# Table loads with buffers and a queue to themselves in a hybrid attention, RWKV-7 and PEER kernel

## The chip, the cores and the metric

The kernel runs on one core of a Trainium2 chip. The metric is the device time in microseconds, as the median of several timed executions; lower is better. One more execution was taken with the hardware profiler. Every number of the trace is from that one.

## What is computed

Two layers of a transformer-like backbone over 512 latent tokens and 256 context tokens of 1024 features. Each layer first mixes tokens (windowed attention, neighbourhood attention and RWKV-7 scans in parallel head groups, one projection out), then runs a PEER layer, which is what this case is about. The PEER layer, cut to what matters:

```python
q = (hb @ wq).reshape(PEER_CHUNK, PEER_HEADS, 2, PEER_QDIM // 2)
s = jnp.einsum('thpd,hpnd->thpn', q, sub_keys).astype(jnp.float32)
sv, si = lax.top_k(s, PEER_TOPK)                 # 16 of 128 keys, twice for each of 8 heads
cand = (sv[:, :, 0, :, None] + sv[:, :, 1, None, :]).reshape(PEER_CHUNK, PEER_HEADS, PEER_TOPK * PEER_TOPK)
best, ci = lax.top_k(cand, PEER_TOPK)            # 16 of the 256 pairs
expert = i1 * PEER_NKEYS + i2                    # one of 128 * 128 experts
gate = jax.nn.softmax(best, axis=-1)
ue = jnp.take(u, expert, axis=0)
ve = jnp.take(v, expert, axis=0)
act = jax.nn.gelu(jnp.einsum('td,thkd->thk', hb, ue).astype(jnp.float32), approximate=False)
return jnp.einsum('thk,thkd->td', (gate * act).astype(hb.dtype), ve)
```

Each token takes 8 x 16 = 128 of the 16384 experts, each a row of the table u and a row of the table v.

## The kernel before

**Two ways to the same sum.** Most tokens are treated densely: the product of all 16384 experts with the token tile is formed and weighted by a matrix W that is zero where an expert was not chosen. In layer 0 these are the four latent tiles of 128 tokens, in layer 1 three of them. The other tiles (the two context tiles in layer 0, the last latent tile in layer 1) are gathered: for each of a token's 128 experts an indirect DMA fetches 128 rows, one per token, of u and v side by side (8 KB each, 1 MB a gather), VectorE forms the dot product with the token (L1472), ScalarE the Gelu (L1474), VectorE multiplies by the gate (L1475) and accumulates v (L1478). Two gathers make one step of this kind (`NQ = 2`). `Gather.tick` is called at fixed places of the dense loops and issues as many gathers as `NTICK` gives for the place, with a high priority: entry 0 in the scores, 1 and 2 in the scored stage, for the first `NFIRST` groups and for the rest, 3 in the value stage.

**The scored stage** (`scored`, called 32 times per layer, a group of four blocks of 128 experts each). A uT row of 1 MB holds two blocks. ScalarE casts a block to its high half (L1311), VectorE subtracts for the low half (L1313), TensorE makes three products per chunk of features into `pa` (`mm3`, L132 to L134: 24 matmuls a block, 512 columns in layer 0, 384 in layer 1), ScalarE applies Gelu (L1317), and the result `aw` is written to the DRAM scratch `ascr` (L1319). Blocks near the end are kept in SBUF instead (`keep`) and multiplied at once by their part of W, a gate row read back from the scratch `wscr` (L1300, L1322): groups 24 to 31 in layer 0, 21 to 31 in layer 1. The half-cast blocks have two buffers each.

**W** is made during the scored stage by `gates`, a generator of five units per dense tile: one of preparation, four that each make W for 32 tokens in eight steps. A step is two one-hot comparisons and one product on VectorE (L1225, L1228), eight matmuls (L1233) and a copy on ScalarE (L1234). At its end a unit writes W, 2 MB, to `wscr` (L1236); W has one buffer. The units are dealt evenly over the first `GSPREAD` groups. In layer 0, `mod_unit` computes one sixth of the next layer's modulation after each fifth group, with four rows of weights each (L167) and matmuls (L159).

**The value stage** runs over the same 128 blocks, kept ones first: a row of v for two blocks (L1364), the same high and low split (L1367, L1369), for blocks not kept `ascr` and `wscr` are read back (L1357, L1359) and multiplied (L1374), and TensorE accumulates into `py` (18 or 24 matmuls of 512 columns a block).

**Rows and queues.** One pool of `NROW` buffers of 8 KB per partition (`Gather.row`) serves the gathers, the tables uT and uv, the gate rows, the modulation rows, the weights of the score stages (L1107), the context's output projection and `load_out`, and the residual rows at the end of a layer. All of these but the gathers are loaded by DMAs that SyncE (SP) issues; so are the writes of `ascr` and `wscr`. Gathers are issued by GpSimd (POOL). A queue is in order: an instruction that waits for its buffer or its data holds everything behind it. The order on each engine, and which free buffer a tile gets, is set when the program is built, by a scheduler that simulates a timeline; no order is written by hand.

## Time and profile before

| | us |
|---|---|
| timed, median of 3 | 5024.15 (5021.28 to 5025.62) |
| profiled execution, its own time | 5011.65 |
| its span, first to last instruction | 5009.9 |
| TensorE matmuls busy | 4425.2 (88%) |
| VectorE busy | 3653.8 (73%) |
| ScalarE busy | 1772.4 (35%) |
| GpSimd busy | 1226.5 (24%) |

The expert stages take about half of the span: layer 0's scored stage from 1096 to 2123 us, its value stage to about 2850, layer 1's scored stage from 3662 to 4464 and its value stage to the end. Busy time says that an engine had an instruction under way; for matmuls the end is modelled, so a count of matmuls times the spacing of an undisturbed stretch tells more. Idle time of an engine is put down to what ended it. The granted clock (PEclk) is TensorE's, as a share of full speed; the DMA share is how much of the 16 DMA engines' time was in use.

### The profile page before, as it was taken

The page shows a single profiled execution, that of the slowest core. Times are in us where ns is not written, and L with a number is a line of the kernel's source. Part 1 is how long each engine was busy: PE and PEld are TensorE (multiplying, and loading weights), DVE is VectorE, ACT ScalarE, POOL GpSimd, SP SyncE. Part 2 cuts the span into 40 slices and gives each one's busy share as a digit, 9 for nine tenths or more (in the row PEclk, how much of TensorE's full clock was granted, in tenths as well). Part 3 has the DMA queues.
Part 4 walks back from the last instruction along what each step waited for, and adds up shares of the span by engine and source line. Part 5 has one row for each costly group of instructions (what it writes and reads, how often), then busy time and mean ns, then how long its engine had stood idle before and what let it go on. Part 6 is the DMA issues. An engine that isn't in the chain of part 4 may idle for free.

```text
span 5009.9 us, 74083 instructions
## 1 busy us (share of the span) xinstructions
PE 4425.2 (88%) x27525; PEld 3669.7 (73%) x27525; DVE 3653.8 (73%) x7587; ACT 1772.4 (35%) x2961; POOL 1226.5 (24%) x1347
## 2 busy tenths in 40 slices
PE   7778887789999988899999886799698997999999
PEld 4557776667787776677788664777588996988787
DVE  3974666889877876677788878557579875676776
ACT  3533245333333332222232354335334332333333
POOL 0025632151112222222222115354031110111120
PEclk9788797899999998999999987889899998999999
DMA  7444654255778888887999834573526885886897
GB/s 268 149 113 124 175 174 157 101 190 199 272 288 340 335 310 309 320 305 274 334 373 351 286 117 120 129 202 103 176 92 219 323 296 223 289 307 251 310 328 243
DMA packets 573481, 1186.55 MB, mean 237 GB/s; under 512 B 62768, under 2 KB 376000, under 8 KB 520384
## 3 DMA queue, kind: packets, MB, share of 16 engines
q1 hardware_dynamic: 506688, 758.39, 45.0%
q0 software_dynamic: 61440, 418.41, 22.6%
q10 hardware_dynamic: 4992, 5.02, 0.4%
q8 instruction: 216, 3.54, 0.3%
q14 instruction: 145, 1.19, 0.1%
HBM read 1005.19 MB, written 176.50 MB: 236 GB/s over the span
## 4 chain that ended last, share of the span: by engine, by line
PE 45%; DVE 16%; issue 15%; DMA 15%; POOL 4%; ACT 3%; SPq 1%; POOLq 0%; ACTq 0%; DVEq 0%
DMA row<-in_uv,eidx 6%; PE py L133 5%; PE py L132 4%; PE py L134 4%; PE pa L132 4%; PE pa L134 4%; PE pa L133 4%; PE pw L1233 3%; DMA row<-in_uT 3%; PE pf L132 2%; POOL row L1461 2%; PE pf L133 2%; PE pf L134 2%; DVE uL L1313 1%; PE pg L840 1%
## 5 line engine op out<-in xcount | busy, mean ns | idle before, releaser
L1461 POOL DMA_INDIRECT row<-in_uv,eidx x384 | 547.4, 1426 | 2350.1 <-DVE accc L1478 1153.0
L132 PE MATMUL pa<-hH,uH 128*128 128x512 f32 (+1 forms) x2048 | 772.8, 377 | 81.9 <-ACT uH L1311 68.0
L134 PE MATMUL pa<-hH,uL 128*128 128x512 f32 (+1 forms) x2048 | 764.6, 374 | 21.1 <-DVE uL L1313 21.0
L133 PE MATMUL pa<-hL,uH 128*128 128x512 f32 (+1 forms) x2048 | 762.8, 372 | 0.0
L133 PE MATMUL py<-vL,GH 128*128 128x512 f32 x1792 | 699.8, 392 | 19.8 <-DVE vL L1369 19.6
L134 PE MATMUL py<-vH,GL 128*128 128x512 f32 x1792 | 697.1, 391 | 0.0
L132 PE MATMUL py<-vH,GH 128*128 128x512 f32 x1792 | 684.3, 392 | 13.3 <-ACT vH L1367 9.2
L1472 DVE SCALAR_TENSOR_TENSOR row<-row,h2c 128x1024 f32<-128x1024 f32 x384 | 473.6, 1236 | 230.3 <-DMA row<-in_uv,eidx 229.8
L132 PEld LDWEIGHTS pa<-hH,uH 128*128 128x128 f32 x2048 | 399.5, 195 | 138.9 <-ACT uH L1311 79.0
L1478 DVE SCALAR_TENSOR_TENSOR accc<-row,dt,accc 128x1024 f32<-128x1024 f32 x384 | 494.2, 1287 | 5.7
L1311 ACT CAST uH<-row 128x1024 fp32r<-128x1024 f32 x256 | 266.2, 1049 | 570.1 <-PE pa L133 435.7
L134 PEld LDWEIGHTS pa<-hH,uL 128*128 128x128 f32 x2048 | 397.4, 194 | 74.6 <-DVE uL L1313 32.7
L1313 DVE TENSOR_TENSOR uL<-row,uH 128x1024 fp32r<-128x1024 f32 x256 | 311.6, 1222 | 161.4 <-ACT uH L1311 156.4
L133 PEld LDWEIGHTS pa<-hL,uH 128*128 128x128 f32 x2048 | 398.8, 195 | 40.1
L133 PEld LDWEIGHTS py<-vL,GH 128*128 128x128 f32 x1792 | 338.6, 189 | 97.2 <-DVE vL L1369 26.9
L132 PEld LDWEIGHTS py<-vH,GH 128*128 128x128 f32 x1792 | 339.2, 189 | 86.0 <-ACT vH L1367 10.0
L134 PEld LDWEIGHTS py<-vH,GL 128*128 128x128 f32 x1792 | 338.8, 189 | 70.0
L1369 DVE TENSOR_TENSOR vL<-row,vH 128x1024 fp32r<-128x1024 f32 x256 | 311.5, 1220 | 13.4 <-ACT vH L1367 13.1
L1367 ACT CAST vH<-row 128x1024 fp32r<-128x1024 f32 x256 | 266.4, 1044 | 15.5 <-DMA row<-in_uv 13.5
L1225 DVE TENSOR_TENSOR oh<-iota,ix 128x512 f16<-128x512 f16 x448 | 171.9, 421 | 135.5 <-PE pw L1233 135.1
L1233 PE MATMUL pw<-og,oh 128*128 128x128 f16 x1792 | 237.9, 297 | 36.4 <-DVE og L1228 19.2
L1233 PEld LDWEIGHTS <-oh 128*128 128x128 f16 x1792 | 190.4, 119 | 76.6 <-DVE og L1228 35.1
(380 smaller groups left out, 8352.1 us busy)
## 6 DMA issues: line engine op xcount, KB each, us to landing
row<-in_uT SPq DMA_DIRECT2D x128, 1024.0 KB
row<-in_uv SPq DMA_DIRECT2D x128, 1024.0 KB
wscr<-W SPq DMA_DIRECT2D x28, 2048.0 KB
wmod<-in_w_mod SPq DMA_DIRECT2D x48, 512.0 KB
row<-in_wq SPq DMA_DIRECT2D x24, 1024.0 KB
ascr<-aw SPq DMA_DIRECT2D x96, 256.0 KB
row<-in_w_mod SPq DMA_DIRECT2D x24, 1024.0 KB
av<-ascr SPq DMA_DIRECT2D x48, 512.0 KB
```

The lines of the kernel that those rows point to most:

```text
L132: mm(out, lh, rh, start=first, stop=False)
L133: mm(out, lh, rl, start=False, stop=False)
L134: mm(out, ll, rh, start=False, stop=last)
L1225: nc.vector.tensor_tensor(oh[:, z], self.iota4, ix[:, z, tt].unsqueeze(1).to_broadcast([P, P, 4]), OP.is_equal)
L1233: nc.tensor.matmul(pw[:, q], oh[:, 1, :, q], og[:, z, :, q], start=z == 0, stop=z == 1)
L1311: nc.scalar.copy(uH, ur)
L1313: nc.vector.tensor_tensor(uL, ur, uH.bitcast(F32), OP.subtract)
L1367: nc.scalar.copy(vH, vr)
L1369: nc.vector.tensor_tensor(vL, vr, vH.bitcast(F32), OP.subtract)
L1461: self.K.nc.gpsimd.indirect_dma_start(out=r, out_offset=None, in_=self.K.i[f"uv{self.l}"], in_offset=bass.IndirectOffsetOnAxis(ap=self.idx ...
L1472: nc.vector.scalar_tensor_tensor(rows[z][:, 0:D], rows[z][:, 0:D], 1.0, self.h[:, a], OP.mult, OP.mult, accum_out=dt[:, z:z + 1])
L1478: nc.vector.scalar_tensor_tensor(acc, v, dt[:, z:z + 1], acc, OP.mult, OP.add)
```

## The change

Five things. The tables uT and uv get two row buffers of their own (`table`), and the common rows go from six to four. The loads of gate rows and of modulation rows are issued by GpSimd, and the writes of `ascr` and `wscr` by ScalarE, all of them by SyncE before. The gate product of a gathered pair moves from one VectorE instruction to two ScalarE ones. The units of W are dealt over 19 groups instead of 22 in layer 0 and 15 instead of 18 in layer 1. And the gathers per tick are set anew: in layer 0 fewer in the scored stage and more in the value stage, with ten instead of twelve groups at the low rate; in layer 1 in the same direction. What is computed stays the same.

```diff
--- before.py
+++ after.py
@@ -33,10 +33,11 @@
 NMIX, NFFN, CV, W0, A0, KKC, KAC, RKC = 0, 8, 16, 61, 69, 77, 81, 85
 NCOL = 89
 LATER = 2000
-NROW = 6
+NROW = 4
+NTAB = 2
 NQ = 2
 MOFF = 500
-GSPREAD = (22, 18)
+GSPREAD = (19, 15)
 LATE = (28, 28)
 NRAW = 4
 TC0 = 6
@@ -54,8 +55,8 @@
 NPRT = 4
 NQKB = {"qs": 3, "kh": 3, "kl": 2}
 
-NTICK = ((2, 1.2, 2.6, 1.75), (0, 0, 1.3, 0.9))
-NFIRST = (12, 3)
+NTICK = ((2, 1.2, 2.3, 1.9), (0, 0, 1.2, 1.0))
+NFIRST = (10, 3)
 FEATS = (12, 13, 4, 0, 5, 1, 6, 2, 7, 3, 14, 8, 9, 10, 11)
 LAT = (0, 1, 2, 3)
 
@@ -164,7 +165,7 @@
             else:
                 if k % 2 == 0:
                     w2 = row().rearrange("p (k n) -> p k n", k=2)
-                    nc.sync.dma_start(w2, src[:, k:k + 2])
+                    nc.gpsimd.dma_start(w2, src[:, k:k + 2])
                 w = w2[:, k % 2]
             for j in range(4):
                 add(j, self.cs[:, k], w[:, j * 256:j * 256 + 256], k == 0, False)
@@ -1233,7 +1234,7 @@
                         nc.tensor.matmul(pw[:, q], oh[:, 1, :, q], og[:, z, :, q], start=z == 0, stop=z == 1)
                 nc.scalar.activation(W[:, :, t4 * 4:t4 * 4 + 4], pw.rearrange("p q i -> p i q"), AF.Copy,
                                      scale=1.0 / GSCALE)
-            nc.sync.dma_start(self.wscr[:, 4 * t + s_], W)
+            nc.scalar.dma_start(self.wscr[:, 4 * t + s_], W)
             yield
 
     def peer_norm(self, l, np_, j, mc, hH, hL, tiles, ps, gat):
@@ -1297,10 +1298,10 @@
 
                 if 4 * g >= P - nres - LATE[l]:
                     wt = gat.row()[:, :4 * nd].rearrange("p (a q t) -> p a q t", q=4, t=32)
-                    nc.sync.dma_start(wt, self.wscr[:, :nd // 32, g * 4:g * 4 + 4, :])
+                    nc.gpsimd.dma_start(wt, self.wscr[:, :nd // 32, g * 4:g * 4 + 4, :])
                 for b in range(4 * g, 4 * g + 4):
                     if b % 2 == 0:
-                        ur2 = gat.row().rearrange("p (z k n) -> p z k n", z=2, k=KC)
+                        ur2 = gat.table().rearrange("p (z k n) -> p z k n", z=2, k=KC)
                         nc.sync.dma_start(ur2, i["uT"][l, b:b + 2].rearrange("z p k n -> p z k n"))
                     if b >= P - nres - (LATE[l] if late else 0):
                         aw = keep[b] = (ar if b >= P - nres else late).tile([P, nd], F32, name=f"ar{b}")
@@ -1316,7 +1317,7 @@
                         self.mm3(pa, uH[:, k], uL[:, k], hH[:, k, :nd], hL[:, k, :nd], k == 0, k == KC - 1)
                     nc.scalar.activation(aw, pa, AF.Gelu)
                     if b not in keep:
-                        nc.sync.dma_start(self.ascr[g, :, b % 4, :nd], aw)
+                        nc.scalar.dma_start(self.ascr[g, :, b % 4, :nd], aw)
                     else:
                         a3 = aw.rearrange("p (a t) -> p a t", t=32)
                         nc.vector.tensor_tensor(a3, a3, wt[:, :, b % 4], OP.mult)
@@ -1360,7 +1361,7 @@
                 for q in range(4):
                     b = g * 4 + q
                     if b % 2 == 0:
-                        vr2 = gat.row().rearrange("p (z d) -> p z d", z=2)
+                        vr2 = gat.table().rearrange("p (z d) -> p z d", z=2)
                         nc.sync.dma_start(vr2, vtab[b * P:(b + 2) * P, :].rearrange("(z p) d -> p z d", p=P))
                     vr = vr2[:, b % 2]
                     vH = vp.tile([P, D], F32R, name="vH", bufs=3)
@@ -1456,6 +1457,9 @@
     def row(self):
         return self.gp.tile([P, 2 * D], F32, name="row", bufs=NROW)
 
+    def table(self):
+        return self.gp.tile([P, 2 * D], F32, name="tab", bufs=NTAB)
+
     def gather(self, a, k):
         r = self.row()
         self.K.nc.gpsimd.indirect_dma_start(out=r, out_offset=None, in_=self.K.i[f"uv{self.l}"],
@@ -1472,7 +1476,8 @@
             nc.vector.scalar_tensor_tensor(rows[z][:, 0:D], rows[z][:, 0:D], 1.0, self.h[:, a], OP.mult, OP.mult,
                                            accum_out=dt[:, z:z + 1])
         nc.scalar.activation(dt, dt, AF.Gelu)
-        nc.vector.tensor_tensor(dt, dt, self.gate[:, a, k:k + NQ], OP.mult)
+        for z in range(NQ):
+            nc.scalar.activation(dt[:, z:z + 1], dt[:, z:z + 1], AF.Copy, scale=self.gate[:, a, k + z:k + z + 1])
         for z in range(NQ):
             v, acc = rows[z][:, D:2 * D], self.acc[:, a]
             nc.vector.scalar_tensor_tensor(acc, v, dt[:, z:z + 1], acc, OP.mult, OP.add)
```

## Rows read from the trace of the kernel before

**Rows 1.** Stretches: busy us (count) of PE, PEld, DVE, ACT, POOL; PEclk, DMA share, GB/s.

```profile
1160.00:1870.00 710.00, 676.10 (x3556) 544.60 (x3557) 568.04 (x1180) 234.77 (x375) 133.22 (x92) 0.97 0.79 296
1870.00:2123.00 253.00, 199.78 (x919) 153.65 (x917) 161.16 (x214) 55.58 (x89) 57.49 (x42) 0.89 0.88 316
2123.00:2500.00 377.00, 355.77 (x1518) 290.89 (x1519) 280.15 (x375) 105.43 (x161) 86.50 (x60) 0.97 0.85 303
2500.00:2826.00 326.00, 326.00 (x1440) 269.93 (x1439) 270.82 (x357) 97.04 (x145) 70.74 (x52) 1.00 0.98 356
3780.00:4200.00 420.00, 390.95 (x2344) 371.65 (x2343) 352.72 (x709) 158.73 (x256) 71.57 (x48) 0.96 0.78 285
4200.00:4270.00 70.00, 44.38 (x273) 40.44 (x273) 32.79 (x62) 18.06 (x29) 1.94 (x2) 0.71 0.54 200
4270.00:4464.00 194.00, 178.97 (x965) 174.08 (x963) 132.84 (x175) 59.04 (x93) 33.08 (x27) 0.95 0.83 299
```

**Rows 2.** The same stretches, instructions of `pa` alone: PE, PEld, ACT.

```profile
1160.00:1870.00 710.00, 546.37 (x2226) 424.80 (x2227) 54.47 (x93) 0.97 0.79 296
1870.00:2123.00 253.00, 188.32 (x773) 149.38 (x771) 19.62 (x33) 0.89 0.88 316
...
3780.00:4200.00 420.00, 324.90 (x1695) 302.85 (x1694) 34.11 (x71) 0.96 0.78 285
4200.00:4270.00 70.00, 27.86 (x145) 26.80 (x145) 2.92 (x6) 0.71 0.54 200
4270.00:4464.00 194.00, 178.97 (x965) 174.08 (x963) 19.31 (x40) 0.95 0.83 299
```

**Rows 3.** The page's costliest groups: busy, mean ns, idle before and what ended it.

```profile
L1478 DVE SCALAR_TENSOR_TENSOR accc<-row,dt,accc 128x1024 f32<-128x1024 f32 x384 | 494.2, 1287 | 5.7
...
L1313 DVE TENSOR_TENSOR uL<-row,uH 128x1024 fp32r<-128x1024 f32 x256 | 311.6, 1222 | 161.4 <-ACT uH L1311 156.4
...
L1225 DVE TENSOR_TENSOR oh<-iota,ix 128x512 f16<-128x512 f16 x448 | 171.9, 421 | 135.5 <-PE pw L1233 135.1
...
L1233 PEld LDWEIGHTS <-oh 128*128 128x128 f16 x1792 | 190.4, 119 | 76.6 <-DVE og L1228 35.1
```

**Rows 4.** Groups by line and form, whole span: one-hot product, Gelu, gate product.

```profile
L1228 DVE TENSOR_TENSOR og<-oh,g 128x1024 f16<-128x1024 f16 x224 | 151.7, 686 | 0.0
...
L1474 ACT ACTIVATE dt<-dt 128x2 f32<-128x2 f32 x192 | 38.8, 202 | 479.2 <-DVE row L1472 479.0
...
L1475 DVE TENSOR_TENSOR dt<-dt,gatec 128x2 f32<-128x2 f32 x192 | 29.8, 155 | 15.0 <-ACT dt L1474 15.0
```

**Rows 5.** The chain of work, 4200 to 4252 us: start, us, what.

```profile
4236.66 6.24 DMA wscr<-W
...
4243.52 6.75 DMA row<-in_uT
```

**Rows 6.** The chain of work, 1865 to 1882 us.

```profile
1869.55 11.34 DMA row<-in_uT
```

**Rows 7.** The chain of work, 4270 to 4464 us, by line; its longest table load.

```profile
by line: DMA row<-in_uT 30.2%; DMA row<-in_uv,eidx 13.7%; issue 10.0%; PE pa L134 8.2%; PE pa L132 7.5%; PE pa L133 7.5%; DVE uL L1313 7.4%; ACT uH L1311 4.4%; DVE accc L1478 3.4%; DMA av<-ascr 2.9%; DVE row L1472 2.6%; DVE ar L1322 1.1%; P
...
4410.47 12.70 DMA row<-in_uT
```

**Rows 8.** SyncE's queue, whom it waited for: us in total, times, longest.

```profile
SPq L1319 <- ACT aw L1317: 665.7, 152, 18.3
...
SPq L1304 <- DVE accc L1478: 221.9, 44, 12.0
```

**Rows 9.** ScalarE's DMA issues at L176: ns, shortest, median and longest.

```profile
L176 ACTq DMA_DIRECT2D mscr<-rmod x24: 483/496/1059, 32.3 to 2063.2; - x24
```

**Rows 10.** The gathers at L1461: issue ns; GpSimd's idle time (us, times); landing.

```profile
L1461 POOL DMA_INDIRECT row<-in_uv,eidx x384: 932/1214/4301, 1017.6 to 4921.8; - x192
...
  DVE accc L1478: 1153.0, 179
...
DMA to landing us min/median/max: 5.4/9.0/16.7
```

## The prediction

> **What bounds the kernel now.** I read the busy times by stage first, then the same stretches for the expert matmuls alone, then the chain of work in the bad stretches, then what SyncE's queue waited for. The stages meant are the two expert stages of each layer: the scored stage (tables uT, product into `pa`) and the value stage (tables uv, product into `py`).
>
> TensorE is the engine to fill. In the second half of layer 0's value stage it is busy for all of the 326 us with 1440 matmuls of 512 columns, so 0.2264 us each [rows 1]; that is my floor price. Layer 1's scored matmuls have 384 columns, so I take three quarters, 0.170 us. A one-hot matmul costs at least its weight load, 0.119 us [rows 3]. With the counts of expert matmuls [rows 2] the floor of each stretch, and what is lost above it, is (matmuls not in `pa` are one-hots, 1024 in layer 0 and 768 in layer 1, and a few others):
> - 1160:1870, layer 0 scored, with one-hots: 2226 x 0.2264 = 504, 1024 x 0.119 = 122, 306 others (modulation) 18 as an estimate between 0 and 306 x 0.119: 644 of 710 us, lost 66.
> - 1870:2123, layer 0 scored, tail: 773 x 0.2264 = 175, others 9: lost 69.
> - 2123:2500, layer 0 value, first half: 1518 x 0.2264 = 344: lost 33.
> - 3780:4200, layer 1 scored, with one-hots: 1695 x 0.170 = 288, 649 x 0.119 = 77: lost 55.
> - 4200:4270, one hole: 145 x 0.170 = 25, 128 x 0.119 = 15: lost 30.
> - 4270:4464, layer 1 scored, tail: 965 x 0.170 = 164: lost 30.
>
> Together 283 us, 6% of the kernel. They hold what the clock costs after a pause: it was granted at 0.71 of full speed in the hole and 0.89 in layer 0's tail, against 1.00 where TensorE never paused [rows 1]. Two limits show in them. One is a queue: in the hole the chain goes from the last write of W (6.24 us) to a table load (6.75 us) [rows 5]. The gate row that needs this last write stands ahead of the table on SyncE, and the table needs nothing of it. The same order starts layer 0's tail with an 11.34 us table load [rows 6], and in layer 1's tail tables fill 30.2% of the chain [rows 7]. SyncE stood 665.7 us before the writes of `ascr`, waiting for the Gelu, and 221.9 us before uT loads because their buffer was still in the hands of a gather's accumulation [rows 8]. The other limit is transfer rate: the stretch with full TensorE moves 356 GB/s at a DMA share of 0.98, and the tail of layer 0 already has a share of 0.88 at 316 GB/s [rows 1].
>
> **The change, part by part.** *Tables in two buffers of their own, SyncE left to them.* A uT load then waits only for the subtraction of the table two loads before. From there to the point where TensorE would starve are some four blocks less one cast and one subtraction: 24 x 0.170 x 4 = 16.3 us in layer 1, less about 1.1 + 1.22 + 1 [rows 3], so some 13 us; in layer 0 some 18. The slowest loads seen there take 12.70 us [rows 7]. So these waits should nearly vanish where rate allows. Hole: 25 of 30 (20 to 30). Layer 1's tail: the chain's 30.2% of 194 us is 59 us of tables, but only 30 us are lost; I take 20 (5 to 30), since gathers are 13.7% of that chain and stay.
>
> *Layer 0's tail* is where rate steps in. It moved 316 GB/s x 253 us = 80 MB. Gathers per pair fall from 2.6 to 2.3, so in its 8 groups about 4.8 gathers of 128 x 8 KB = 1.05 MB leave: 75 MB. At 356 GB/s that is 210 us, with full TensorE 184. I take 220, a gain of 33 (5, if the rate stays as it is, to 43).
>
> *Layer 0's value stage* takes what left: 0.15 more per pair on 64 pairs, 9.6 gathers, 10 MB. It moved 303 x 377 + 356 x 326 = 230 MB; 240 MB at 356 GB/s is 674 us against 703 now and a floor of 670. Gain 12 (-15 to 29): I stay well below the 29, since the stage would run at the highest rate seen without a pause.
>
> *Writes of W and of `ascr` on ScalarE's queue.* 28 + 180 issues. The nearest row is ScalarE's own write of `mscr`, 0.496 us [rows 9]: 103 us over both scored stages. Behind each stands the next cast. ScalarE is busy 235 of 710 and 159 of 420 us there [rows 1], and casts run a block ahead of TensorE (5.4 or 4.1 us), so I price this at 0; without that cover it is 103 us at most. A gain is possible, since a write leaves as soon as its data is there, where SyncE came later; it is counted with the hole.
>
> *Gate rows and modulation rows on GpSimd's queue.* 8 + 11 + 24 = 43 loads. Nearest row for the issue is a gather's, 1.21 us [rows 10]: 52 us of GpSimd, which is busy 133 of 710 us. What counts is what stands behind them: gathers, which share four buffers with them instead of six with tables as well. A gather lands 9.0 us after its issue (5.4 to 16.7) [rows 10]. A gate row holds its buffer for a group, so three are left for gathers then: a gather held for 16 us gives one in 5.3 us, and 4.6 per group of 21.7 us asks for one in 4.7. Gathers will lag a little in layer 0's tail; the lag moves into the value stage and is part of the 12 above. I take 0, and the far end goes to the rival below.
>
> *Four gather rows instead of six elsewhere.* The context's projection, both score stages and the layer's end use the same rows for weights and residuals, and there SyncE's order stays. No row prices it. Bounds: 0, and some 8 places where a load of 4 to 7 us comes one buffer too late, 40 us; I take -8. Nothing there gets a buffer or a freer queue, so a gain is excluded.
>
> *Gate product on ScalarE.* 192 VectorE instructions of 0.155 us and 15.0 us of idle before them go, 45 us; 384 of about 0.2 us come on ScalarE, 77 us [rows 4]. VectorE is short only beside the one-hots, where about 130 of the 384 gathers lie, so 65 pairs x 0.155 = 10 us. The chain from dot to accumulation gets one more ScalarE step of 0.2 us, under the next pair's dots.
>
> *One-hots over 19 and 15 groups.* A W step costs VectorE 2 x 0.421 + 0.686 = 1.53 us and TensorE 8 x 0.119 = 0.95. Layer 1 had 96/18 = 5.3 steps per group, now 6.4. VectorE per group of four blocks: 4 x 1.22 + 6.4 x 1.53 + 2.4 gathers x 2 x 1.29 = 21 us, with choosing, an estimate, some 25, against 16.3 + 6.1 = 22.4 on TensorE; before, 5.3 x 1.53 + 4.9 + 2.6 x 2.6 and choosing gave some 24 against 21.4 [rows 3, 4]. So VectorE leads during the one-hots in both, and 15 x 25 + 3 x 16.3 = 424 against 18 x 24 = 432: nearly a swap. With the 10 us of the gate product I take 8 in 1160:1870 (-25 to 30) and 5 in 3780:4200 (-15 to 20).
>
> **Sum:** 25 + 20 + 33 + 12 + 8 + 5 - 8 = 95 us. The profiled execution took 5011.65 us (span 5009.9), so 4917; the timed median, 5024.15, is 12.5 us (0.25%) above it: 4929. I predict **4930 us**.
>
> **The rivals.**
> *Rate, not queue.* For: the share of 0.88 in layer 0's tail, and more gathers in a stage already at 0.98. Then layer 0 gives nothing; the hole (25), half of layer 1's tail (10) and -8 remain: 27 us, 4997. Against: the hole has a share of only 0.54, layer 1's tail 0.83.
> *The moves change nothing.* If the tables wait for transfers and not for SyncE's order, then taking 28 + 180 + 43 = 251 issues off SyncE takes them off an engine that is not on TensorE's path, and the time stays at 5024. For: single table loads of 11 and 12 us [rows 6, 7]. Against: SyncE's 665.7 us before `ascr` are 152 waits of 4.4 us each for a Gelu, with the table behind them [rows 8]; that is order. The Trainium skill (DMA: Bandwidth & Descriptors, section Issuing engines are not separate DMA queues) states this rival as a rule: issuing from several engines only saves the sequencer's issue time, usually small. By that rule the sum would be nothing; the trace agrees with it about the transfers, but not about the waits in order.
> *Nearly all comes back.* If both tails reach their floors and VectorE follows: the upper bounds less little, 30 + 30 + 43 + 25 + 25 + 12 - 5 = 160: 4864.
> *Slower: GpSimd's queue becomes what SyncE's was.* A row load waits for a free row among four, and all gathers stand behind it; modulation matmuls stand in TensorE's order, the gate product of kept blocks in VectorE's. GpSimd's wait for a row is now 1153.0 us in 179 waits, 6.4 us each [rows 10]. If each of the 43 loads costs TensorE more than 95 / 43 = 2.2 us, the gain is gone; at 6.4 us each it is 275 us, and if half of that lies beside TensorE's other work, 138 are lost: 5067. Against: gate rows are needed by VectorE only, and modulation six times.
>
> **Chances.** Forecast 0.55, nearly all 0.15, rate 0.14, nothing 0.07, slower 0.09. Range 4860 to 5020: 4864 at its lower end, the rate case within, nothing and slower mostly out. About 0.2% (10 us) is what a measurement of this kernel can tell from no change: faster 0.84, same 0.07, slower 0.09.
>
> **What would show it.** uT loads fall out of the chain in both tails and no SyncE instruction but a table, a column vector or the value stage's own loads stands before one; the stretch with the last W has no hole of 15 us; the share in layer 0's tail rises towards 0.98. Wrong would be: TensorE waiting for modulation rows or for VectorE's products with a gate row, gather rows as the reason of SyncE's waits in the projection, or unchanged tails at a DMA share of 0.9.

## The result, and the profile after

The changed kernel takes 4954.2 us against 5022.7 us before (medians), 68 us less. The ratio of the runs side by side is 0.9873 [0.9849, 0.9897], which is 1.3% or 64 us. The forecast was 4930 us. The profiled execution has a span of 4950.8 us against 5009.9 us, so 59 of the 68 us can be looked for in the two traces.

I cut both traces at ScalarE's casts of tables, which stand in the same order in both kernels: the fifth `uH` cast of a layer (the first group of four blocks is done), the first `vH` cast, and the 125th. "Start" is what lies ahead of the first cut, "between" what lies from layer 0's last value group to layer 1's first group; 32 to 34 us stand behind the last cut. The changed kernel's lines have numbers one to five higher than the same lines before (L1304 becomes L1305, L1461 becomes L1465, the three products L132 to L134 become L133 to L135). Stage times in us, for every kernel of this document:

| kernel | start | L0 scored | L0 value | between | L1 scored | L1 value | span |
|---|---|---|---|---|---|---|---|
| before | 1158.8 | 963.8 | 703.1 | 917.8 | 720.9 | 513.3 | 5009.9 |
| after | 1148.0 | 911.3 | 708.3 | 899.1 | 709.7 | 542.1 | 4950.8 |
| e1 tables only | 1142.2 | 934.3 | 710.7 | 909.5 | 696.2 | 537.0 | 4962.0 |
| e2 gate rows on SyncE | 1143.8 | 922.6 | 708.3 | 915.6 | 698.6 | 547.6 | 4968.6 |
| e3 16 late blocks | 1141.9 | 888.8 | 718.5 | 907.7 | 677.5 | 554.9 | 4921.6 |
| e4 two buffers for W | 1141.4 | 892.1 | 710.9 | 905.4 | 696.5 | 548.0 | 4926.5 |
| e5 queues only | 1161.5 | 949.2 | 698.0 | 902.9 | 709.8 | 521.2 | 4975.2 |
| e6 value rows shared | 1141.8 | 910.6 | 709.0 | 906.4 | 709.2 | 525.8 | 4935.1 |
| e7 shared, 16 late | 1141.7 | 886.4 | 717.9 | 915.0 | 680.2 | 523.5 | 4897.8 |
| e8 gate product on VectorE | 1143.4 | 907.0 | 707.3 | 900.8 | 689.7 | 530.5 | 4911.1 |
| e9 before, product on ScalarE | 1170.4 | 961.4 | 692.4 | 909.4 | 710.4 | 521.7 | 4997.9 |
| e10 old rates | 1138.3 | 926.3 | 708.3 | 905.6 | 704.8 | 539.1 | 4954.7 |
| e11 shared, late, VectorE | 1150.7 | 893.8 | 723.5 | 916.0 | 680.1 | 502.0 | 4898.6 |
| e12 as e11, two for W | 1142.9 | 873.2 | 723.1 | 916.1 | 688.5 | 511.8 | 4889.3 |

The stretches of the changed kernel that answer to [rows 1] (us, busy us and count of PE, PEld, DVE, ACT, POOL; granted clock, DMA share, GB/s): layer 0's scored stage in three, its value stage in two, layer 1's scored stage in three, its value stage in two:

```profile
1148.00:1808.00 660.00, 643.53 (x3359) 514.95 (x3358) 530.06 (x1126) 241.68 (x429) 136.78 (x107) 0.99 0.83 302
1808.00:1882.00 74.00, 49.22 (x286) 39.85 (x285) 41.85 (x83) 20.90 (x38) 5.00 (x5) 0.68 0.50 189
1882.00:2059.00 177.00, 169.78 (x843) 133.47 (x842) 115.69 (x141) 53.52 (x101) 52.49 (x41) 0.99 0.93 341
2059.00:2417.00 358.00, 352.19 (x1536) 289.60 (x1536) 306.21 (x384) 124.62 (x235) 108.25 (x73) 0.99 0.98 356
2417.00:2767.00 350.00, 329.81 (x1419) 264.10 (x1420) 288.57 (x357) 112.02 (x207) 98.14 (x60) 1.00 0.97 351
3667.00:4125.00 458.00, 423.43 (x2520) 404.67 (x2519) 373.10 (x822) 180.93 (x310) 83.50 (x45) 0.97 0.74 266
4125.00:4189.00 64.00, 41.92 (x276) 37.38 (x275) 32.35 (x67) 19.90 (x33) 3.03 (x3) 0.68 0.46 171
4189.00:4376.00 187.00, 176.24 (x985) 173.00 (x983) 129.90 (x161) 65.28 (x120) 47.92 (x36) 0.98 0.83 301
4376.00:4678.00 302.00, 270.41 (x1137) 214.98 (x1138) 263.72 (x334) 113.30 (x222) 87.30 (x57) 0.98 0.98 361
4678.00:4918.00 240.00, 240.00 (x1060) 198.72 (x1060) 134.01 (x178) 86.92 (x118) 0.00 (x0) 1.00 0.71 221
```

There is still a hole in layer 1 (4125 to 4189, clock 0.68), and layer 0 now has one too (1808 to 1882); outside them the scored stages pause less, with clocks of 0.97 to 0.99 where [rows 1] has 0.89 to 0.97. Layer 1's value stage is two different halves: 57 instructions on GpSimd (gathers) and then none.

What the change was for is seen at the first of the three expert products, before and then after (busy us, mean ns, TensorE's idle us before it and what ended them):

```profile
L132 PE MATMUL pa<-hH,uH 128*128 128x512 f32 (+1 forms) x2048 | 772.8, 377 | 81.9 <-ACT uH L1311 68.0 <-ACT aw L1317 13.1
```

```profile
L133 PE MATMUL pa<-hH,uH 128*128 128x512 f32 (+1 forms) x2048 | 760.7, 371 | 43.4 <-ACT aw L1318 28.1 <-ACT ar L1318 15.2
```

Before, TensorE stood 68.0 us for the casts of uT tables; in the changed kernel it never does. What it waits for now is a Gelu that has to empty a product, 15.2 us of it the Gelu of a kept block (`ar`), which e3 explains. In the value stages it is the other way round:

```profile
L132 PE MATMUL py<-vH,GH 128*128 128x512 f32 x1792 | 684.3, 392 | 13.3 <-ACT vH L1367 9.2
```

```profile
L133 PE MATMUL py<-vH,GH 128*128 128x512 f32 x1792 | 589.8, 394 | 50.9 <-ACT vH L1368 41.9
```

TensorE's wait for the casts of value tables rises from 9.2 to 41.9 us (36.0 in e1, 7.7 in e5). Late loads explain a part at most: ScalarE's casts waited 13.5 us for them before and 23.1 us now.

SyncE's queue in the changed kernel (whom it waited for, us in total, times, longest):

```profile
SPq L1305 <- DVE uL L1314: 1166.5, 95, 62.6
SPq L1365 <- DVE vL L1370: 556.1, 115, 12.6
```

The waits of [rows 8] are gone from it. It waits most for the subtractions that free a table's buffer, which means that it is ahead. How far ahead is seen at the table loads of the scored stages, before and then after (shortest, median and longest ns, first and last start):

```profile
L1304 SPq DMA_DIRECT2D row<-in_uT x128: 367/383/11981, 1091.5 to 4441.3; - x128
```

```profile
L1305 SPq DMA_DIRECT2D tab<-in_uT x128: 367/368/3094, 742.7 to 4355.2; - x128
```

The first table leaves at 742.7 us instead of 1091.5, since no other work uses its buffer; the first expert matmul starts at 1030 us instead of 1098.

### The profile page after: what moved, and what is told of

Read it like the earlier page. It is cut to its first block, busy times and chain, and to the rows that moved or that the text cites. A ratio compares the mean times of both kernels' runs of the same rounds, so it can differ in the third digit from the quotient of the medians.

```text
span 4950.8 us, 73840 instructions
## 1 busy us (share of the span) xinstructions
PE 4408.5 (89%) x27525; PEld 3651.6 (74%) x27525; DVE 3639.2 (74%) x7395; ACT 1870.6 (38%) x3349; POOL 1322.9 (27%) x1390
## 5 line engine op out<-in xcount | busy, mean ns | idle before, releaser
L1465 POOL DMA_INDIRECT row<-in_uv,eidx x384 | 593.9, 1547 | 1529.4 <-DVE accc L1483 1125.7
L133 PE MATMUL pa<-hH,uH 128*128 128x512 f32 (+1 forms) x2048 | 760.7, 371 | 43.4 <-ACT aw L1318 28.1
L135 PE MATMUL pa<-hH,uL 128*128 128x512 f32 (+1 forms) x2048 | 760.0, 372 | 23.7 <-DVE uL L1314 23.5
L134 PE MATMUL pa<-hL,uH 128*128 128x512 f32 (+1 forms) x2048 | 753.8, 368 | 0.0
L134 PE MATMUL py<-vL,GH 128*128 128x512 f32 x1792 | 700.7, 393 | 11.8 <-DVE vL L1370 11.6
L135 PE MATMUL py<-vH,GL 128*128 128x512 f32 x1792 | 696.1, 390 | 0.0
L133 PE MATMUL py<-vH,GH 128*128 128x512 f32 x1792 | 589.8, 394 | 50.9 <-ACT vH L1368 41.9
L1483 DVE SCALAR_TENSOR_TENSOR accc<-row,dt,accc 128x1024 f32<-128x1024 f32 x384 | 497.7, 1296 | 36.8 <-ACT dt L1480 29.3
L1312 ACT CAST uH<-tab 128x1024 fp32r<-128x1024 f32 x256 | 268.7, 1050 | 657.9 <-PE pa L134 622.2
L133 PEld LDWEIGHTS pa<-hH,uH 128*128 128x128 f32 x2048 | 393.1, 192 | 92.6 <-ACT aw L1318 35.1
L135 PEld LDWEIGHTS pa<-hH,uL 128*128 128x128 f32 x2048 | 392.3, 192 | 80.3 <-DVE uL L1314 33.9
L133 PEld LDWEIGHTS py<-vH,GH 128*128 128x128 f32 x1792 | 336.4, 189 | 132.1 <-ACT vH L1368 53.3
L134 PEld LDWEIGHTS pa<-hL,uH 128*128 128x128 f32 x2048 | 392.4, 192 | 40.3 <-issue 0.4
L134 PEld LDWEIGHTS py<-vL,GH 128*128 128x128 f32 x1792 | 338.0, 189 | 95.3 <-DVE vL L1370 25.7
L1314 DVE TENSOR_TENSOR uL<-tab,uH 128x1024 fp32r<-128x1024 f32 x256 | 318.7, 1246 | 115.6 <-ACT uH L1312 115.3
L135 PEld LDWEIGHTS py<-vH,GL 128*128 128x128 f32 x1792 | 337.4, 188 | 69.8
L1370 DVE TENSOR_TENSOR vL<-tab,vH 128x1024 fp32r<-128x1024 f32 x256 | 308.6, 1220 | 18.2 <-ACT vH L1368 18.0
L1379 ACT CAST GH<-G 128x512 fp32r<-128x512 f32 (+1 forms) x180 | 102.9, 572 | 518.9 <-PE py L134 365.5
L1226 DVE TENSOR_TENSOR oh<-iota,ix 128x512 f16<-128x512 f16 x448 | 171.8, 423 | 144.1 <-PE pw L1234 144.0
L1368 ACT CAST vH<-tab 128x1024 fp32r<-128x1024 f32 x256 | 261.0, 1044 | 23.1 <-DMA tab<-in_uv 23.1
```

What stands on the lines that cost most here:

```text
L133: mm(out, lh, rh, start=first, stop=False)
L134: mm(out, lh, rl, start=False, stop=False)
L135: mm(out, ll, rh, start=False, stop=last)
L1226: nc.vector.tensor_tensor(oh[:, z], self.iota4, ix[:, z, tt].unsqueeze(1).to_broadcast([P, P, 4]), OP.is_equal)
L1312: nc.scalar.copy(uH, ur)
L1314: nc.vector.tensor_tensor(uL, ur, uH.bitcast(F32), OP.subtract)
```

## The experiments

Each ratio is to the kernel before, run beside it. Two things hold for all of them. Built with 22 and 18 in place of 19 and 15, the changed kernel's program has the same order on TensorE, ScalarE, GpSimd and SyncE and one exchanged subtraction on VectorE, so dealing the one-hots anew does nothing here. And the order of a program is the planner's, so an edit of a few instructions can reorder thousands; e9 moves one small product and changes the time by 17 us, and a difference of that size can be the order's.

**e1, the tables' buffers alone.** The kernel before with `NROW = 4`, `NTAB = 2` and

```
-   ur2 = gat.row()...
+   ur2 = gat.table()...
-   vr2 = gat.row()...
+   vr2 = gat.table()...
```

> The kernel before with the one edit that uT and uv get two row buffers of their own and the common rows go from six to four; SyncE keeps every load and write, gathers per tick and gate product as before. Theory A (the buffers were the lever): tables no longer wait for a gather's accumulation (221.9 and 322.6 us of SyncE's waits before), so most of the 68 us of the whole change is here already: 4955 to 4975. Theory B (the order on SyncE's queue was the lever): a table still stands behind the writes of ascr and the gate rows, and the four common rows make gate rows wait longer in front of it: 5005 to 5030.

Measured: 4964.6 us, 0.9906 [0.9877, 0.9935], 47 us by the ratio. The buffers alone bring most of the gain, as theory A has it, and TensorE's wait for the casts of uT tables, 68.0 us before, is gone with them:

```profile
L133 PE MATMUL pa<-hH,uH 128*128 128x512 f32 (+1 forms) x2048 | 761.3, 372 | 42.1 <-ACT aw L1318 25.7 <-ACT ar L1318 16.3
```

**e5, the queues alone.** The kernel before with the writes of W and `ascr` on ScalarE's queue, gate rows and modulation rows on GpSimd's, tables still in shared buffers:

```
-   nc.sync.dma_start(wt, self.wscr...)
+   nc.gpsimd.dma_start(wt, self.wscr...)
-   nc.sync.dma_start(w2, src[:, k:k + 2])
+   nc.gpsimd.dma_start(w2, src[:, k:k + 2])
-   nc.sync.dma_start(self.wscr..., W)
+   nc.scalar.dma_start(self.wscr..., W)
-   nc.sync.dma_start(self.ascr..., aw)
+   nc.scalar.dma_start(self.ascr..., aw)
```

> The kernel before with the three queue moves alone (scratch writes on ScalarE's queue, gate rows and modulation weights on GpSimd's); the tables still share the six row buffers, and nothing else is changed. Theory A (buffers): with the gathers in the tables' way the order of SyncE's queue is worth no more than what the tables' own buffers left over, 68 less 53 us, so 0 to 15 us faster than before: 5003 to 5018 us, and SyncE's waits for row buffers (221.9 us before, for the accumulates) grow as those for the scratch writes go. Theory B (order): the 665.7 us that SyncE stood before the scratch writes are what the tables were late by, and either half of the change alone would cure it: 4965 us or so, with the last groups of layer 0's scored part at 21.8 us each.

Measured: 4976.4 us, 0.9928 [0.9908, 0.9948], 36 us: between the two theories. SyncE's waits moved as theory A had it (before: 221.9 us [rows 8]):

```profile
SPq L1304 <- DVE accc L1478: 469.4, 50, 21.5
...
SPq L1304 <- DVE uL L1313: 240.3, 22, 50.4
```

but the tables still came earlier:

```profile
L132 PE MATMUL pa<-hH,uH 128*128 128x512 f32 (+1 forms) x2048 | 772.0, 377 | 51.9 <-ACT uH L1311 32.6 <-ACT aw L1317 19.2
```

So order and buffers are two causes of one wait: the moves alone take 35 of its 68.0 us, the buffers alone all of it. If their gains in time added, they would make 0.9906 x 0.9928 = 0.983, more than the whole change brought (0.987). The intervals leave room for no difference; if there is one, something in the change takes back some 0.4%. The Trainium skill (DMA: Bandwidth & Descriptors, section Issuing engines are not separate DMA queues) says that issuing from several engines saves only the sequencer's issue time. This run goes beyond that: the moves came with 36 us, and with 35 us less of TensorE's wait for uT tables.

**e2, gate rows back on SyncE** in the changed kernel:

```
-   nc.gpsimd.dma_start(wt, self.wscr...)
+   nc.sync.dma_start(wt, self.wscr...)
```

> The changed kernel with the 19 gate rows loaded by SyncE again, all else as changed. Theory A: the 196 us that GpSimd stood in layer 1 before its first gate row, with no gather issued, was this load's place in GpSimd's order; without it gathers run through layer 1's scored stage, its value stage falls from 542 us back to about 515, and tables, two ahead, cover part of SyncE's wait for W: 4925 to 4945. Theory B: the value stages are slower because more gathers were dealt to them and the transfers are at their rate; then layer 1's value stage stays at 540 and SyncE's wait for the last W costs a hole: 4955 to 4985.

Measured: 4952.8 us, 0.9878 [0.9849, 0.9907]: no difference from the changed kernel, and layer 1's value stage did not shorten, so theory A falls. The gate rows (`L1301`) on GpSimd show in the changed kernel (idle before them by reason):

```profile
L1301 POOL DMA_DIRECT2D row<-wscr x19: 1067/1079/1209, 1874.6 to 4357.1; - x19
its engine sat idle before it (us, times) until:
  DMA wscr<-W: 196.4, 1
  DVE accc L1483: 78.6, 11
```

The 196.4 us are layer 1's: the first gate row waits there for the last write of W and the gathers stand behind it. That looked like the price of GpSimd's queue. It isn't one: in e2 GpSimd stands as long (196.5 us) without the gate row on its queue. Its next gather waits there for a buffer whose accumulation VectorE does only behind its product with the first gate row. The place in the queue costs nothing that the time shows.

**e3, 16 late blocks for 28** in the changed kernel, so that the first gate row, and the first tile of a kept block, are wanted three groups later:

```
-LATE = (28, 28)
+LATE = (16, 16)
```

> The changed kernel with 12 blocks fewer kept in each layer (LATE 28 to 16), so that the first gate row is needed three groups later (24 and 27 become 27 and 24 as first kept groups in layers 0 and 1, from 24 and 21). Theory A (the last W steps are held together by the first gate row, one write of W after the other): the runs of 24 W steps in one group go, each costs some 30 us now, and GpSimd is blocked for less: 4895 to 4925. Theory B (the rate of W steps is short of VectorE or TensorE): the hole only moves three groups on, and 12 more blocks go through ascr: 4950 to 4965.

Measured: 4925.0 us, 0.9827 [0.9798, 0.9855]. First why, from the changed kernel's chain of work in the hole of layer 1 (start us, us, what):

```profile
4144.30 7.94 DMA wscr<-W
...
4152.32 0.60 ACT W L1235
4152.93 0.04 issue
4152.97 1.12 PE pw L1234 x8
...
4161.16 6.26 DMA wscr<-W
...
4176.34 6.27 DMA wscr<-W
4182.63 0.04 POOLq L1301
...
4183.34 0.54 POOL row L1301
```

W has a single buffer. Each of its units of eight one-hot steps (`L1226` to `L1235`) must be written to memory (6.3 to 7.9 us) before the next copy into it, and the last units stand one behind the other ahead of the first kept group. Three writes take 20.5 us of this group; TensorE, which does a few one-hots beside them, stands for 22.1 us in it (64.00 - 41.92). Its longest wait is the last, and it is not for the gate row, which needs all of W, but for a Gelu:

```profile
PE pa L133 <- ACT ar L1318: 7.5, 1, 7.5
```

This is the Gelu of the first kept block (`ar`). It starts at 4182.63 us, as soon as the third write has landed and before the gate row is issued (4183.34). ScalarE waited for writes of W in two places (us, times, both layers):

```profile
  ACT W L1235: 36.7, 11
  ACT ar L1318: 12.7, 2
```

The kernel shows why a Gelu should wait for a write: the late kept blocks come from a pool (`ar2`) that is opened where the pool of the one-hots has been closed (`sg.close()`), so their tiles lie in memory that W had. The prediction and the plan of this experiment have the gate row alone in mind; e3 delays both, and it is the trace that tells them apart. In e3, the same 75 us of layer 0 from the start of its group 24, and four groups of layer 1, where the changed kernel has its holes (columns as above):

```profile
1801.00:1876.00 75.00, 72.42 (x433) 57.38 (x432) 53.41 (x88) 26.25 (x47) 13.05 (x14) 1.00 0.89 322
4097.00:4186.00 89.00, 89.00 (x573) 86.62 (x572) 49.40 (x83) 36.63 (x56) 0.00 (x0) 1.00 0.56 206
```

No pause in layer 1, and the granted clock 1.00 where it was 0.68. Both scored stages together win 54.7 us (table); 23 are lost again in the value stages, where three groups more have to be reloaded in each layer.

**e4, two buffers for W** in the changed kernel (room from 12 kept blocks for 16 in layer 1 and single buffers for four small tiles):

```
-   W = pool.tile([P, P, 32], F32, name="W", bufs=1)
+   W = pool.tile([P, P, 32], F32, name="W", bufs=2)
```

> The changed kernel with two buffers for W instead of one; for the room, four tiles of preparation have one buffer instead of two and layer 1 keeps 12 instead of 16 blocks in its first pool. Theory A (a W step waits for the last write of W to land, 6 to 11 us per unit, 28 units): no run of 24 steps behind one another, the hole shrinks from some 30 us to under 10 in each layer, GpSimd stands less before its first gate row: 4890 to 4920. Theory B (steps are paced by VectorE and TensorE): W ends no earlier, 4945 to 4960.

Measured: 4928.3 us, 0.9826 [0.9795, 0.9857]. The largest group falls from 74.5 to 46.8 us in layer 0 and from 63.7 to 37.7 in layer 1. The time lies between the two theories. What TensorE still stands for in layer 1's group is one wait of 12.3 us, for the first kept Gelu, which waits 11.1 us for a write of W. So the hole has two parts: W's single buffer, and the kept tiles in W's memory, both made dear by when the units are due.

**e6, layer 1's value stage shares rows again**, every second table pair in a gather's row buffer:

```
-   vr2 = gat.table()...
+   vr2 = (gat.row() if not wc and b % 4 == 0 else gat.table())...
```

> The changed kernel, but in layer 1's value part every second table load takes a gather's row buffer, so that the gathers can't run ahead of the groups they were dealt to: two per group through the part, where the changed kernel has four per group in the first half and none in the second. Theory A (bunching): the changed kernel's 29 us of loss in layer 1's value part (513 to 542 us) comes from the groups with four gathers, where VectorE has more than a group's work; spread, each group fits beside TensorE's 16.3 us, and the part comes back to 513 to 522 us: 4926 to 4935 us in all. Theory B (rate): the part is longer for another reason, its eight gathers more than before or the tables' being loaded but two deep; then the part stays at 540 us and the time at 4950 us.

Measured: 4940.2 us, 0.9861 [0.9839, 0.9883]. The value stage's halves before, and in e6 (columns as above):

```profile
4464.00:4729.00 265.00, 257.37 (x1120) 210.65 (x1121) 189.64 (x257) 96.55 (x146) 38.64 (x29) 0.99 0.80 281
4729.00:4978.00 249.00, 245.71 (x1082) 202.48 (x1081) 187.53 (x262) 89.61 (x132) 35.47 (x22) 1.00 0.93 322
```

```profile
4377.00:4654.00 277.00, 262.59 (x1118) 214.36 (x1119) 193.73 (x246) 102.29 (x178) 47.57 (x33) 0.97 0.79 278
4654.00:4903.00 249.00, 247.02 (x1082) 202.35 (x1082) 194.71 (x263) 95.05 (x161) 36.95 (x24) 1.00 0.98 338
```

In the changed kernel VectorE was busy for 263.7 of the first 302 us and 134.0 of the other 240; here 193.7 and 194.7. Bunching is real, and without it the stage gets back 16.3 of the 28.8 us that it lost; TensorE's wait for casts of value tables in it falls from 18.6 to 5.5 us. 12.5 remain. In the whole time the gain is 6 us by the ratio (14 by the medians), too little to be told from none by these intervals.

**e7, e6 and e3 together.**

> The same sharing in layer 1's value part, together with 16 blocks kept late instead of 28. If the hole before the first kept group and the bunched gathers are two separate losses, the gains add: 4925 (with 16 late blocks alone) less 20 to 28 us, 4897 to 4905 us. If both are one and the same limit (VectorE's total work, which then comes back elsewhere), the second brings little: 4915 to 4925 us.

Measured: 4909.4 us, 0.9795 [0.9773, 0.9818], between the two forecasts. The gains add roughly: value stage -18.6 us, scored stages -54.4 us against the changed kernel.

**e8, the gate product back on VectorE** in the changed kernel:

```
-   for z in range(NQ):
-       nc.scalar.activation(dt[:, z:z + 1], dt[:, z:z + 1], AF.Copy, scale=self.gate[:, a, k + z:k + z + 1])
+   nc.vector.tensor_tensor(dt, dt, self.gate[:, a, k:k + NQ], OP.mult)
```

> The changed kernel with the gathers' gate product back on VectorE: one product of 0.154 us for each pair of rows there in place of two of 0.284 us on ScalarE. Theory A: the part is worth nothing by itself, since 192 x 0.15 = 29 us of VectorE's work is spread over 3000 us in which VectorE mostly has slack: 4950 to 4960 us. Theory B: where VectorE sets the pace (the groups with four gathers, some 60 of them) its 0.15 us a pair and the trip from ScalarE to VectorE and back count: 5 to 12 us slower, 4960 to 4966 us.

Measured: 4922.8 us, 0.9837 [0.9801, 0.9873]. Both theories fell: it is not slower but faster, 18 us by the ratios and 31 by the medians (the intervals of e8 and of the changed kernel overlap). The kernel of e8 has the edits of e1 and of e5 together, and its ratio is the 0.983 that those two make if they add. So the product on ScalarE seemed to be the part that takes back.

**e9, the same part alone, put into the kernel before** (the lines of e8 the other way round).

> The kernel before with one part of the change alone: the gathers' gate product on ScalarE, two products of 0.284 us for a pair of rows in place of one of 0.155 us on VectorE. Theory A (the product costs on ScalarE): 384 x 0.284 = 109 us of work come to the engine that casts every table and empties every product, and its Gelus leave later, so the kernel gets slower by about what putting it back won in the changed kernel, 20 to 35 us: 5040 to 5050 us. Theory B (what was won there came with the order that the planner found, not with the product): no loss here, 5005 to 5020 us.

Measured: 5000.7 us, 0.9967 [0.9953, 0.9981]: not slower but 17 us faster. The time is under both forecasts. Theory A falls as a rule for the whole kernel. What is left is the order that the planner finds with the product on one engine or the other; that it decides is argued, not shown. One stage alone has one sign: layer 1's value stage, 8.4 us longer with the product on ScalarE here (513.3 to 521.7), 11.6 in e8's pair (530.5, 542.1), 21.5 in e11's (502.0, 523.5). TensorE's waits in that stage are, in e7 and in e11, which differ in the product alone (us in total, times, longest):

```profile
PE py L134 <- DVE vL L1370: 12.8, 9, 3.2
PE py L133 <- ACT vH L1368: 5.7, 1, 5.7
```

```profile
PE py L133 <- ACT vH L1368: 6.0, 1, 6.0
PE py L134 <- DVE vL L1370: 0.4, 1, 0.4
```

They differ by 12.1 of the 21.5 us. The rest is TensorE's busy time for the same matmuls, 509.6 us at a granted clock of 0.98 and 500.3 us at 1.00.

The product on ScalarE is 384 instructions of 0.284 us (the Copy with a column of scales; the page's group of 192 pairs), 109 us:

```profile
L1480 ACT ACTIVATE dt<-dt,gatec x384: 277/284/298, 1043.8 to 4661.1; 128x1 f32<-128x1 f32 x192
its engine sat idle before it (us, times) until:
  ACT dt L1478: 3.6, 11
who waited for it (us, times):
  DVE accc L1483: 29.3, 44
```

VectorE waited 29.3 us in 44 times for it, where it waited 15.0 us for the Gelu before [rows 4].

**e10, the old rates of gathers** in the changed kernel:

```
-NTICK = ((2, 1.2, 2.3, 1.9), (0, 0, 1.2, 1.0))
-NFIRST = (10, 3)
+NTICK = ((2, 1.2, 2.6, 1.75), (0, 0, 1.3, 0.9))
+NFIRST = (12, 3)
```

> The changed kernel with the old rates of gathers (2.6 and 1.75 per pair of blocks in layer 0, 1.3 and 0.9 in layer 1). Theory A: fewer gathers are left for layer 1's value part, whose bunched half gets shorter by 6 of 60 accumulations (some 4 us), and layer 0's value part, which transfers bound, moves 8 gathers less (some 6 us); the scored parts give back as much, since the accumulations are VectorE's work there too: 4945 to 4958 us. Theory B: the lower rates in the scored parts are what brought the gain of layer 0's last groups; then those get 10 to 20 us longer and the time is 4960 to 4970 us.

Measured: 4953.4 us, 0.9863 [0.9846, 0.9879]. No difference in the time, as theory A has it, but not by its terms: layer 0's scored stage is 15 us longer, the start 10 and layer 1's stages 8 shorter; layer 0's value stage, with eight gathers fewer, is not shorter by a microsecond. Theory B's part is there too: layer 0's last groups, 24 to 31, take 262.7 us for 251.8.

**e11, e7 with the product on VectorE.**

> The changed kernel with three things put right: 16 late blocks, the shared row buffers in layer 1's value part, and the gate product on VectorE. Theory A (the product costs on ScalarE wherever it stands): 20 to 30 us under the kernel with the first two, 4909 us: 4880 to 4890 us. Theory B (the order that the planner found): the gain of the product vanishes with the other order, 4900 to 4915 us.

Measured: 4896.2 us, 0.9753 [0.9736, 0.9769], 13 us by medians and 21 by ratios under e7: between the theories. Layer 1's value stage gains 21.5 us and is now shorter than before the change; layer 0's scored and value stages and the start lose 22.

**e12, e11 with two buffers for W** (12 kept blocks, as in e4).

> As the one before, with two buffers for W as well (12 kept blocks instead of 16 in layer 1 for their room). If the hole is W's single buffer and 16 late blocks have already spread the steps, two buffers bring 0 to 5 us more; four kept blocks fewer give 4 more writes and reloads, about nothing. If the wait for W's write still costs in every unit (5 us in each of some 5 units), 10 to 20 us: 4865 to 4880 us.

Measured: 4882.4 us, 0.9724 [0.9707, 0.9740], 14 us under e11, 137 us under the kernel before and 72 under the changed one: the best of these. The gain is of the second kind that was expected, 10 to 20 us. Layer 0's scored stage is 873.2 us, and none of the groups beside the one-hots is a hole any more.

## Where the prediction was right and where not

The time, 4954, lies within the range and 24 us above the forecast of 4930; the sign and the first cause (tables held up by buffers and by SyncE's order) are right, as TensorE's wait for uT tables shows: 68.0 us before, 32.6 with the moves alone (e5), none with the buffers alone (e1). The terms of the sum are mostly not right. Of the signs that were named, no uT load stands in the chain of layer 1's tail any more, and the DMA share in layer 0's last seven groups rose, to 0.93; but the stretch with the last W kept a hole of over 15 us. Forecast gains beside the stage times of the two traces, in us:

| step | forecast | measured |
|---|---|---|
| hole in layer 1 | 25 | 4.4 (group 68.1 to 63.7) |
| layer 1's tail | 20 | 8.2 (last 10 groups, 195.6 to 187.4) |
| layer 0's tail | 33 | -10.1 (241.7 to 251.8) |
| layer 0's value stage | 12 | -5.2 |
| layer 0, with the one-hots | 8 | 62.5 (722.1 to 659.6) |
| layer 1, with the one-hots | 5 | -1.4 |
| four rows elsewhere | -8 | 29.5 (start 10.8, between 18.7) |
| layer 1's value stage | no term | -28.8 |
| sum | 95 | 59.1 |

- **The hole.** The step failed. I read the chain of [rows 5], a write of W of 6.24 us with a table load behind it, as SyncE's order. The table load went, and the hole stayed: the writes were the price themselves, since the next unit waits for W's only buffer and the first kept Gelu for W's memory. e2 leaves it untouched, e3 takes it away, e4 about half of its pauses. What I should have looked for is how many such writes stand one behind another and what else waits for the memory that they hold.
- **Layer 0's tail.** Two things in one term. Its last seven groups gained 18.4 us (195.8 to 177.4), with the DMA share rising from 0.88 to 0.93, and as forecast it took the buffers and the lower rate of gathers together. By the buffers, groups 25 to 30 fell from 167.2 to 139.0 us (136.3 in e1, 142.9 in e10, 173.2 in e5). The last group rose from 28.6 to 38.4 us, and with the old rates to 61.3 (e1) and 54.5 (e10), where TensorE waits 11.8 and 9.5 us for rows of the modulation. Its first group lost 28.5 us (45.9 to 74.4), because the 24 last one-hot steps landed there, with 24.8 us of pauses; the steps' floor is 24 x 0.95 = 22.8 us, and these left the stage before. It is the hole of layer 1 in layer 0, which the prediction did not see coming.
- **Layer 0 with the one-hots.** Mis-sized: of the 62.5 us, 22.8 are those steps, so about 40 were gained where 8 stood. I had put the tables' waits into the tails and the hole alone; e1 finds nearly the whole of it too (its group 24 starts 662 us after the first cut, the changed kernel's 660), so the buffers are enough for it, and VectorE's product and the deal, from which I had worked the 8, are not needed. TensorE's idle time in the stage falls from 44.3 to 16.5 us, of which some 12 before were waits for tables (2.2 us, and some 10 of one that ends just behind the stage); which other waits the buffers took away, and how, is not shown.
- **Layer 0's value stage.** The bytes were mis-sized: 251 MB moved in its 708.3 us where I had 240 (128 gathers were issued in it for 108 before, 20 more and not 9.6), at 354 GB/s, and 251 MB at the 356 of [rows 1] are 704 us. The stage did run at its highest rate, but that rate is not shown to set the time: e10 has 120 gathers and 247 MB there and takes the same 708.3 us. TensorE's wait for casts of its tables rose from 9.2 to 23.2 us.
- **Four rows elsewhere.** The reason that excluded a gain failed: "nothing there gets a buffer". The next stage's tables do: their first load goes out 349 us earlier, and the first blocks are computed beside the scores, with 17 gathers issued before the first cut where there were 5. In e1 the start is 16.6 us shorter, in e5 not at all; the 18.7 us between the layers appear in both, 8 and 15.
- **Layer 1's value stage.** No term stood for it. The buffers that the tables left were also the brake that dealt the gathers out, about two to a group; without it they run nearly four to a group until they are used up, and VectorE is busy for 0.87 of the time in one half and 0.56 in the other (e6). Beside it stands the gate product, which I had priced as a relief of VectorE: in this stage it makes the time longer on ScalarE (e7 to e11: 21.5 us).
- **Gate product.** The count was right, the instruction 0.284 us for the 0.2 assumed. Its effect on the whole has either sign: 17 us faster in the kernel before, 18 to 21 slower in the changed one. What of that is the product and what the other order of the program stays open outside layer 1's value stage.
- **Priced at nothing:** the issues on ScalarE and GpSimd and the dealing of the one-hots. The first holds in so far as e5 gains with all of them in it (a write of W takes 0.326 us to issue there). The deal does nothing, since the order of the program doesn't change.
- **The rivals.** "Rate, not queue" is refuted by e1, which gains 47 us at the old rates, 29.5 us of it in layer 0's scored stage; the rate has its part in layer 0's last group. "The moves change nothing" is refuted by e5. "GpSimd's queue becomes what SyncE's was" has its waits in the trace, at the row for gathers (busy, mean ns, idle and its reasons):

```profile
L1465 POOL DMA_INDIRECT row<-in_uv,eidx x384 | 593.9, 1547 | 1529.4 <-DVE accc L1483 1125.7 <-PE pm L160 147.2 <-DVE cf L1178 55.6
```

The 147.2 us are gathers behind rows that the modulation holds, and 196.4 stand before a gate row (e2). Both are long, and little of either reached TensorE: it waited 1.6 us for a modulation row (10.7 before), and 10.7 us in layer 1's last ten groups for subtractions, at least one of them (3.6 us) behind a gather that VectorE stood for.

That the sum came out near the time is luck in good part: misses of 21, 12, 43, 17, 6 and 29 us on one side stand against 54 and 38 on the other.

## What to carry to other kernels

Own buffers for a stream do two things at once: its loads run ahead, into stages that stand before it, and whatever shared the buffers loses a brake, which shows as work bunched in one half of a stage; look for both. A chain that goes through a write and then a load is no proof that the load's queue is at fault: count the writes that follow each other, and ask what frees their buffer and which other tiles lie in its memory, before the load is blamed. Where a planner orders the program, an edit of small instructions is priced by pairs in more than one surrounding, since the order of the program may be worth more than the instruction.

## What the runs showed of the hardware

A gate row's issue takes 1.08 us on GpSimd where it took 0.37 on SyncE. With the tables in buffers of their own a gather's issue has a median of 1.64 to 1.68 us (the changed kernel and every run that has them) and 1.15 to 1.21 with shared ones (before, e5, e9), with landings of about 9 us in both; why was not tested, and GpSimd has the time. In the two holes TensorE stood for 24.8 and 22.1 us and was granted 0.68 of full speed over the group; without the pauses (e3) it was granted 1.00, in layer 1 with the same 24 one-hot steps spread over four groups.
